# Stick-breaking attention inside a fused encoder block: the layout of the stored values, the order of the first and last steps, and a third output buffer

## The chip, the cores and the metric

The kernel runs on one core of a Trainium2 chip. The metric is the device time of one execution in microseconds (us); the kernel before takes 1874.46 us in the median of three runs (1873.33 to 1877.96).

## What is computed

One layer of an encoder trunk on 1024 tokens of width 1024, in float32. The part that the change touches is branch A, an attention with 16 heads of 64 channels whose weights come from a stick-breaking product instead of a softmax:

```python
h = rmsnorm(x, ln1_g) * (1 + sc1) + sh1
q, k, v, cb, cc, cx, ga, gb = split(h @ w_in)
q, k = rmsnorm(q per head), rmsnorm(k per head)
z = q @ k.T / sqrt(64)                       # strictly causal, s < t
a[t, s] = sigmoid(z[t, s]) * prod_{s < j < t} (1 - sigmoid(z[t, j]))
y_a = a @ v
y_b = cb * causal_dwconv3(cc * cx)
merged = sigmoid(ga) * (y_a @ w_branch_a) + sigmoid(gb) * (y_b @ w_branch_b)
x = x + g1 * (merged @ w_out)
x = x + g2 * swiglu_ffn(rmsnorm(x) * (1 + sc2) + sh2)
```

## The kernel before, in words

Every float32 matrix is split into a high and a low part, and a product is three TensorE (PE) matmuls (high by high, high by low, low by high). The kernel is a row of stages. The first computes the input norm and the projections of v (its first half) and k; then come q, the convolution inputs and the gates; then the attention stage; then branch A's projection, the output projection and the feed-forward part. Most intermediate results go to DRAM and come back (the tiles named `d_...`).

**Attention.** A step is one head and one block of 128 queries, so there are 128 steps, 8 to a head. `att_scores` multiplies queries and keys into PSUM (z, L774 and L775), ScalarE (ACT) takes a sigmoid of the negated score (L776), and VectorE (DVE) forms the running product along the keys with one scan (L780). The attention weight of a key is the difference of two neighbouring running products. The kernel never forms it: it multiplies the running product with the difference of neighbouring value rows, v[t] - v[t-1], and adds the last value. `load_v` (L719 to L725) therefore loads the values twice from DRAM, as `va` (shifted) and `vb`, for two heads at a time; `att_dv` (L727 to L735) subtracts them on DVE (1024 elements in each partition) and splits the difference into `vt`. `att_trans` transposes the running product on PE (L795) and splits it (ACT L798, DVE L799) two steps later; `att_av` multiplies it with `vt` every second step (L810, L811), adds the last value (`vlast`, L815), and DVE puts the sum into the tile `oy` (L817), of which there are two; the SP queue writes it to `d_ya` (L819).

**Values.** `d_v` (L68) holds the values of heads 0 to 7 as 1025 rows of 512 floats, those of heads 8 to 11 and 12 to 15 as 1025 rows of 256; row 0 is zero (L420). A store writes whole rows: 2 KB pieces from `finish_v` (L407, ACT's queue, first stage), 1 KB pieces from the fillers (L889, SP's queue, inside the attention stage). A load takes 128 columns of each row, in pieces of 512 bytes. `load_vlast` reads the last row of each block of 128 into `vl`, in the buffer tagged `va`.

**Fillers.** `fillers` is a generator of matmul work that attention does not need at once: the second half of the v projection (32 pieces of 12 matmuls of 256 columns, L884 to L886), the cb projection and branch B's projection (64 pieces of 6 matmuls of 512 columns each, L865 to L867). Ten pieces (`HEAD`, L941) run ahead of the first step; `fill` (L946) lets the rest through in proportion to the attention work done, up to `FILL - TAIL`, and what is left follows the last value product (`lastav`, L973).

**Order.** The order of each engine's queue is fixed when the program is built: among the instructions that are ready by the planner's timeline, the one of highest priority goes first (`schedule_with_timeline_sim`, L1559). Priority follows the order of the code, and `tc.high_priority()` puts attention ahead of the fillers. `tc.issue_after(x)` adds an edge that keeps the instructions of its block behind x on x's own engine. Every queue then runs strictly in its order: an instruction that waits holds up all that is behind it on its engine. SP issues nearly all loads and stores of the attention stage, ACT's queue those of the first stages.

In step s of `attention()` (L826): the keys and queries of the next head are loaded at the head's first step (L832), `va` and `vb` of the next pair of heads at s % 16 = 10 and 11 (L835 to L837), the difference is formed at s % 8 = 5 or 6 (L838), `load_vlast(1)` stands at s = 54. Before the loop (L954 to L962) come `load_vlast(0)`, the two value loads, the keys of head 0, the first difference, and the ten filler pieces.

Of the kernel before, what the change touches and what calls it, by code (L numbers as in the profile page):

```python
# [16 lines left out]
P = 128  # L17
# [11 lines left out]
def block_kernel(tc, x, x_t, cols, ada_1, ada_2, ada_row, w_q, w_kv, w_v1, w_cg, w_a, w_b, w_o, w_g, w_u, w_d, out):  # L29
# [8 lines left out]
    def nm(s):  # L38
        uid[0] += 1
        return f"{s}_{uid[0]}"  # L40
# [27 lines left out]
    d_v = [drp.tile([T + 1, n], F32, name=f"d_v{n}_{e}") for e, n in enumerate((512, 256, 256))]  # L68
# [310 lines left out]
    def finish_k(ps, i, ch):  # L379
# [13 lines left out]
        hl_ = ap.tile([P, 2, 512], F32R, tag="vs", bufs=3, name=nm("khl"))  # L393
# [7 lines left out]
    def finish_v(ps, i):  # L401
        vs = ap.tile([P, 512], F32, tag=("vs", "qn")[i % 2], bufs=3 - i % 2, name=nm("vs"))
        if i % 2:
            nc.vector.tensor_copy(out=vs, in_=ps)
        else:
            nc.scalar.activation(vs, ps, AF.Copy)
        nc.scalar.dma_start(d_v[0][1 + i * P:1 + (i + 1) * P], vs)  # L407
# [11 lines left out]
    for e in range(3):  # L419
        nc.scalar.dma_start(d_v[e][0:1], mk[0:1, :d_v[e].shape[1]])  # L420
# [298 lines left out]
    def load_v(h, e):  # L719

        pr = h // 2
        d, c0 = (d_v[0], pr * P) if h < 8 else (d_v[1 + (h - 8) // 4], pr % 2 * P)
        t_ = ("vb", "va")[e]
        vab[t_] = bp.tile([P, KT, P], F32, tag=t_, bufs=1, name=nm(t_))
        lastld[0] = nc.sync.dma_start(vab[t_], d[e:T + e, c0:c0 + P].rearrange("(i p) d -> p i d", p=P))  # L725
# [11 lines left out]
    def load_vlast(e):  # L737

        vl = bp.tile([8, 512], F32, tag="va", bufs=1, name=nm("vl"))
        for d, c in (((0, 0),), ((1, 0), (2, 256)))[e]:  # L740
            nc.sync.dma_start(vl[:, c:c + d_v[d].shape[1]], d_v[d][1:].rearrange("(i p) d -> i p d", p=P)[:, P - 1])
        return vl
# [60 lines left out]
    def att_av(h, g):  # L803
# [9 lines left out]
        yv = bp.tile([DH, 256], F32, tag="oy", bufs=2, name=nm("oy"))  # L813
# [12 lines left out]
    def attention():  # L826

        steps = [(h, i) for h in range(H) for i in (LAST if h == H - 1 else ORDER)]
        for s in range(len(steps) + DAV):
            if s < len(steps):  # L830
                h, i = steps[s]
                if s % 8 == (0 if h else 3) and h + 1 < H:  # L832
                    with tc.issue_after(lastld[0].ins):
                        att_load(h + 1)
                if s % 16 in (10, 11) and h + 1 < H:  # L835
                    with tc.issue_after(lastz[0].ins):
                        load_v(h + 1, 11 - s % 16)  # L837
                if s % 8 == (6 if h % 2 else 5) and h + 1 < H:  # L838
                    att_dv(h + 1)
                if s == 54:  # L840
                    with tc.issue_after(lastld[0].ins):
                        vl = load_vlast(1)
                if s == 56:
                    turn_vlast(1, vl)
                yield from att_scores(h, i)
            if s >= DAV:
                h, i = steps[s - DAV]
                if s % 2 != DAV % 2:
                    yield from att_av(h, i // 2)
            if 0 <= s - 2 < len(steps):  # L850
                yield from att_trans(*steps[s - 2])
# [17 lines left out]
    def fillers():  # L869
        for e in range(2):  # L870
# [5 lines left out]
            for i in range(8):  # L876
# [12 lines left out]
                nc.sync.dma_start(d_v[1 + e][1 + i * P:1 + (i + 1) * P], vs)  # L889
# [51 lines left out]
    HEAD, TAIL = 10, 20.0  # L941
# [12 lines left out]
    with tc.high_priority():  # L954
        vl = load_vlast(0)
        turn_vlast(0, vl)
        load_v(0, 1)
        load_v(0, 0)
        att_load(0)
        att_dv(0)  # L960
        for j in range(HEAD):
            next(fl)  # L962
    at_ = attention()
    while True:
# [4 lines left out]
        ta += ca_  # L969
        with tc.issue_after(lastz[0].ins):  # L970
            fill(min(ta * ratio, FILL - TAIL))
    fill(FILL - TAIL)
# [590 lines left out]
```

## Time and profile before

| | before |
|---|---|
| median of 3 runs | 1874.46 us (1873.33 to 1877.96) |
| the profiled execution's own time | 1876.28 us |
| its span, first to last instruction | 1874.5 us |
| PE busy | 1822.7 us, 97% of the span |
| DVE busy | 1351.5 us, 72% |
| ACT busy | 795.0 us, 42% |
| PE's granted clock, mean | 0.990 |
| DMA | 357.98 MB, 191 GB/s in the mean |

Busy PE time is modelled from pipelined matmuls, so a busy PE is not PE at its peak; idle time of PE is real. In a timeline row the columns are the start, the time taken, the engine, the line and operation, what it writes and reads, and in brackets how long the engine stood idle before it and for whom. In a windows row they are the stretch, its length, each engine's busy time with its count of instructions, PE's granted clock (1.00 is full), the mean busy share of the 16 DMA engines and their rate. "x3" is the count of merged instructions. Attention fills the stretch from about 571 to 1040 us.

### The profile page before, as it was taken

To read this page: it belongs to the slowest core of one execution; us is meant where nothing else is said; L and a number is where in the kernel's file an instruction comes from. 1 tells how busy PE (TensorE), PEld (TensorE's weight loads), DVE (VectorE), ACT (ScalarE), POOL (GpSimd) and SP (SyncE) were. 2 spreads that over 40 slices of the span, in tenths; PEclk is the share of its full clock that TensorE was granted. 3 is DMA by queue.
4 is the path that set the end of the run, shared out by engine and by line. 5 is a ranking of instruction groups with operands and counts; after the bars stand their busy time and mean duration, and the time that the engine had idled before them with its cause. 6 is when DMAs were issued, how large, how long until landed. Compare 5 with 4: busy or idle time off the path is not lost. (4 is left out here: it accounts for less than half of the span.)

```text
span 1874.5 us, 24882 instructions
## 1 busy us (share of the span) xinstructions
PE 1822.7 (97%) x8829; PEld 1510.6 (81%) x8829; DVE 1351.5 (72%) x1946; ACT 795.0 (42%) x1494; POOL 369.4 (20%) x277
## 2 busy tenths in 40 slices
PE   7999999999998999998999999989999999999999
PEld 5787778888878988887888888867888888878887
DVE  6873877778963888786888544579987787744776
ACT  4342553333343656555656311564344334422321
POOL 1043328324230000000000000104544454300000
PEclk9999999999999999999999999999999999999999
DMA  9588452226739466678653636424443334388866
GB/s 390 201 306 304 163 174 78 74 99 238 275 135 271 124 191 163 185 189 276 164 162 109 206 125 221 130 79 169 152 185 135 147 146 171 121 317 325 289 225 224
DMA packets 156417, 357.98 MB, mean 191 GB/s; under 512 B 15467, under 2 KB 54653, under 8 KB 154118
## 3 DMA queue, kind: packets, MB, share of 16 engines
q1 hardware_dynamic: 114048, 289.09, 46.2%
q10 hardware_dynamic: 41238, 63.64, 9.7%
q0 software_dynamic: 1008, 3.67, 0.5%
q8 instruction: 70, 1.15, 0.2%
q14 instruction: 53, 0.43, 0.1%
HBM read 245.71 MB, written 110.63 MB: 190 GB/s over the span
## 5 line engine op out<-in xcount | busy, mean ns | idle before, releaser
L780 DVE TENSOR_TENSOR_SCAN pt<-pt,mk 128x128 f32<-128x128 f32 (+7 forms) x128 | 172.1, 1350 | 31.2 <-ACT pt L776 30.8
L776 ACT ACTIVATE pt<-z,rq 128x512 f32<-128x512 f32 (+2 forms) x192 | 108.0, 580 | 95.1 <-PE z L775 62.7
L127 PE MATMUL e<-big,whi 128*128 128x512 f32 x352 | 137.6, 391 | 3.2 <-ACT whi L1056 2.5
L129 PE MATMUL e<-big,wlo 128*128 128x512 f32 x352 | 137.3, 390 | 0.9 <-DVE wlo L1057 0.8
L128 PE MATMUL e<-big,whi 128*128 128x512 f32 x352 | 137.0, 389 | 0.0
L118 POOL TENSOR_SCALAR rs_m<-ss 128x1 f32<-128x1 f32 x8 | 2.2, 281 | 674.3 <-ACT xn L1195 674.3
L132 DVE TENSOR_TENSOR c<-e,c 128x512 f32<-128x512 f32 x138 | 92.8, 687 | 52.6 <-PE e L129 50.8
L127 PE MATMUL pj<-big,whi 128*128 128x512 f32 x320 | 125.2, 391 | 0.5 <-DVE c L132 0.4
L128 PE MATMUL pj<-big,whi 128*128 128x512 f32 x320 | 124.7, 390 | 0.0
L129 PE MATMUL pj<-big,wlo 128*128 128x512 f32 x320 | 124.4, 390 | 0.0
L1390 PE MATMUL e<-whi,f 128*128 128x512 f32 (+1 forms) x319 | 121.8, 382 | 1.5 <-DMA f<-d_f 1.5
L1391 PE MATMUL e<-wlo,f 128*128 128x512 f32 (+1 forms) x319 | 121.8, 382 | 0.0
L1392 PE MATMUL e<-whi,f 128*128 128x512 f32 (+1 forms) x319 | 121.6, 382 | 0.0
L132 DVE TENSOR_TENSOR c<-pj,c 128x512 f32<-128x512 f32 x140 | 93.3, 683 | 33.4 <-PE pj L129 33.2
L290 PE MATMUL pj<-whi,big 128*128 128x512 f32 x352 | 110.7, 401 | 3.1 <-ACT big L273 3.0
L132 POOL TENSOR_TENSOR ws<-raw,raw 128x512 f32<-128x512 f32 x40 | 56.9, 1424 | 288.1 <-DMA raw<-w_cg 145.0
L466 ACT ACTIVATE whi<-raw 128x512 fp32r<-128x512 f32 x116 | 72.5, 630 | 92.1 <-PE pj L128 39.6
L799 DVE TENSOR_TENSOR atl<-tr,ath 128x512 fp32r<-128x512 f32 (+1 forms) x192 | 99.9, 549 | 15.6 <-ACT ath L798 14.1
L132 DVE TENSOR_TENSOR wlo<-raw,whi 128x512 fp32r<-128x512 f32 x116 | 87.5, 759 | 31.9 <-ACT whi L466 31.9
L798 ACT ACTIVATE ath<-tr 128x512 fp32r<-128x512 f32 (+1 forms) x192 | 86.4, 489 | 47.8 <-PE o L810 25.6
L127 PE MATMUL e<-rh,whi 128*128 128x512 f32 x264 | 104.3, 395 | 2.4 <-ACT rh L1073 2.4
L128 PE MATMUL e<-rl,whi 128*128 128x512 f32 x264 | 104.6, 396 | 1.2 <-DVE rl L132 1.2
(255 smaller groups left out, 5043.5 us busy)
## 6 DMA issues: line engine op xcount, KB each, us to landing
f<-d_f SPq DMA_DIRECT2D x77, 512.0 KB, 4.4
d_f<-fs SPq DMA_DIRECT2D x70, 512.0 KB, 3.4
raw<-w_cg SPq DMA_DIRECT2D x40, 512.0 KB, 3.7
raw<-w_u SPq DMA_DIRECT2D x26, 512.0 KB, 3.2
raw<-w_g SPq DMA_DIRECT2D x25, 512.0 KB, 3.4
ad<-ada ACTq DMA_DIRECT2D x19, 512.0 KB, 4.7
ada<-ada SPq DMA_DIRECT2D x8, 1024.0 KB, 9.2
d_t<-ts SPq DMA_DIRECT2D x16, 512.0 KB, 4.9
```

Source lines behind the costliest of these rows:

```text
L127: nc.tensor.matmul(ps, wh[:, k, :], fh[:, k, :], start=(k == 0), stop=False)
L128: nc.tensor.matmul(ps, wh[:, k, :], fl[:, k, :], start=False, stop=False)
L129: nc.tensor.matmul(ps, wl[:, k, :], fh[:, k, :], start=False, stop=(k == 3))
L132: eng.tensor_tensor(out=out, in0=a, in1=b, op=op)
L290: nc.tensor.matmul(ps, a, b, start=(k == 0 and q == 0), stop=(k == KT - 1 and q == 2))
L776: nc.scalar.activation(pt[:, off + s0:off + s0 + m], z[:, :m], AF.Sigmoid, scale=rq[:, 1, i, h:h + 1])
L780: nc.vector.tensor_tensor_scan(out=pt[:, rev], data0=pt[:, rev], data1=mk[:, rev], initial=1.0, op0=ALU.mult, op1=ALU.max)
L798: nc.scalar.activation(th[:, :nb, c0:c0 + P], src, AF.Copy)
L799: nc.vector.tensor_tensor(out=tl[:, :nb, c0:c0 + P], in0=src, in1=th[:, :nb, c0:c0 + P].bitcast(F32), op=ALU.subtract)
L1390: nc.tensor.matmul(o, sh, w[0][:, c], start=(j == 0), stop=False)
L1391: nc.tensor.matmul(o, sh, w[1][:, c], start=False, stop=False)
L1392: nc.tensor.matmul(o, sl, w[0][:, c], start=False, stop=(j == NJ - 1))
```

## The change

The values now lie in DRAM as `d_v[n, 129, 8, 128]`: for each pair of heads, partition p holds in row p + 1 the values of tokens p, 128 + p, 256 + p and so on, 128 floats of each, 4 KB in one piece. A load (`vb` from rows 1 to 128, `va` from rows 0 to 127) is 128 pieces of 4 KB. A store now writes pieces of 512 bytes. Row 0, which `va` needs in partition 0, is a copy of row 128 moved on by one block: `put_before` copies it from DRAM to DRAM on SP's queue, after the last store of each group, three times in all. `vl` gets a buffer of its own, `oy` a third one, and the tiles of the first stage that hold k and half of the v stores a fourth.

Ahead of the loop the keys of head 0 are now loaded first, then the values; the first difference moves to step 2; 16 filler pieces instead of 10 run first, and the rest is thinned (`FILL` less 1.3 for each of the 16, `TAIL` 10). In the loop the value loads stand at s % 16 = 6 and 7, for the pair that follows, and the loads and differences stand in a block tied behind `lastz`, the latest score matmul. After the last step, each yield of the remaining value products and transposes lets one more piece of 1.3 through.

```diff
-    d_v = [drp.tile([T + 1, n], F32, name=f"d_v{n}_{e}") for e, n in enumerate((512, 256, 256))]
+    d_v = [drp.tile([n, P + 1, KT, P], F32, name=f"d_v{n}_{e}") for e, n in enumerate((4, 2, 2))]
...
-        hl_ = ap.tile([P, 2, 512], F32R, tag="vs", bufs=3, name=nm("khl"))
+        hl_ = ap.tile([P, 2, 512], F32R, tag="vs", bufs=4, name=nm("khl"))
...
-        vs = ap.tile([P, 512], F32, tag=("vs", "qn")[i % 2], bufs=3 - i % 2, name=nm("vs"))
+        vs = ap.tile([P, 512], F32, tag=("vs", "qn")[i % 2], bufs=4 - i % 2 * 2, name=nm("vs"))
...
-        nc.scalar.dma_start(d_v[0][1 + i * P:1 + (i + 1) * P], vs)
+        nc.scalar.dma_start(d_v[0][:, 1:, i].rearrange("r p d -> p r d"), vs.rearrange("p (r d) -> p r d", d=P))
...
+    def put_before(e):
+
+        nc.sync.dma_start(d_v[e][:, 0, 1:], d_v[e][:, P, :KT - 1])
+
+    put_before(0)
...
-        d, c0 = (d_v[0], pr * P) if h < 8 else (d_v[1 + (h - 8) // 4], pr % 2 * P)
+        d = d_v[0][pr] if h < 8 else d_v[1 + (h - 8) // 4][pr % 2]
...
-        lastld[0] = nc.sync.dma_start(vab[t_], d[e:T + e, c0:c0 + P].rearrange("(i p) d -> p i d", p=P))
+        lastld[0] = nc.sync.dma_start(vab[t_], d[e:P + e])
...
-        vl = bp.tile([8, 512], F32, tag="va", bufs=1, name=nm("vl"))
+        vl = bp.tile([8, 512], F32, tag="vl", bufs=1, name=nm("vl"))
...
-        yv = bp.tile([DH, 256], F32, tag="oy", bufs=2, name=nm("oy"))
+        yv = bp.tile([DH, 256], F32, tag="oy", bufs=3, name=nm("oy"))
...
         for s in range(len(steps) + DAV):
+            flush[0] = s >= len(steps)
             if s < len(steps):
...
-                if s % 16 in (10, 11) and h + 1 < H:
-                    with tc.issue_after(lastz[0].ins):
-                        load_v(h + 1, 11 - s % 16)
-                if s % 8 == (6 if h % 2 else 5) and h + 1 < H:
-                    att_dv(h + 1)
+                with tc.issue_after(lastz[0].ins) if s else ExitStack():
+                    if s == 2:
+                        att_dv(0)
+                    if s % 8 == (6 if h % 2 else 5) and h + 1 < H:
+                        att_dv(h + 1)
+                    if s % 16 in (6, 7) and s + 16 < len(steps):
+                        load_v(2 * (s // 16) + 2, 7 - s % 16)
...
-                nc.sync.dma_start(d_v[1 + e][1 + i * P:1 + (i + 1) * P], vs)
+                nc.sync.dma_start(d_v[1 + e][:, 1:, i].rearrange("r p d -> p r d"), vs.rearrange("p (r d) -> p r d", d=P))
+                if i == 7:
+                    put_before(1 + e)
...
-    HEAD, TAIL = 10, 20.0
+    HEAD, TAIL = 16, 10.0
+    FILL -= 1.3 * HEAD
...
         turn_vlast(0, vl)
+        att_load(0)
         load_v(0, 1)
         load_v(0, 0)
-        att_load(0)
-        att_dv(0)
         for j in range(HEAD):
             next(fl)
     at_ = attention()
+    flush, nfl = [0], 0
     while True:
...
         ta += ca_
+        nfl += flush[0]
         with tc.issue_after(lastz[0].ins):
-            fill(min(ta * ratio, FILL - TAIL))
-    fill(FILL - TAIL)
+            fill(min(ta * ratio, FILL - TAIL) + 1.3 * nfl)
```

More of the change, by code (lines that the diff above doesn't have):

```diff
@@ L419, in block_kernel @@
     for e in range(3):
-        nc.scalar.dma_start(d_v[e][0:1], mk[0:1, :d_v[e].shape[1]])
+        n = d_v[e].shape[0]
+        nc.scalar.dma_start(d_v[e][:, 0:1, 0].rearrange("r p d -> p r d"), mk[0:1, :n * P].rearrange("p (r d) -> p r d", d=P))
+    def put_before(e):
+        nc.sync.dma_start(d_v[e][:, 0, 1:], d_v[e][:, P, :KT - 1])
+    put_before(0)
     def more():
@@ L737, in load_vlast @@
     def load_vlast(e):
-        vl = bp.tile([8, 512], F32, tag="va", bufs=1, name=nm("vl"))
+        vl = bp.tile([8, 512], F32, tag="vl", bufs=1, name=nm("vl"))
         for d, c in (((0, 0),), ((1, 0), (2, 256)))[e]:
-            nc.sync.dma_start(vl[:, c:c + d_v[d].shape[1]], d_v[d][1:].rearrange("(i p) d -> i p d", p=P)[:, P - 1])
+            n = d_v[d].shape[0]
+            nc.sync.dma_start(vl[:, c:c + n * P].rearrange("i (r d) -> i r d", d=P), d_v[d][:, P].rearrange("r i d -> i r d"))
         return vl
```

## The prediction

> **What bounds the kernel now.** The page comes first, to see whether one engine carries the span.
>
> ```profile
> span 1874.5 us, 24882 instructions
> PE 1822.7 (97%) x8829; PEld 1510.6 (81%) x8829; DVE 1351.5 (72%) x1946; ACT 795.0 (42%) x1494; POOL 369.4 (20%) x277
> ```
>
> PE does, and the change removes no matmul, so all it can win is time in which PE stands idle or runs slow: idle is 1874.5 - 1822.7 = 51.8 us. The windows view of the attention stage and PE's waits in it say how much lies there and for whom PE stood.
>
> ```profile
> 560.00:600.00 40.00, 34.89 (x225) 31.79 (x224) 10.27 (x15) 9.32 (x20) 0.00 (x0) 0.96 0.86 252
> 600.00:1040.00 440.00, 424.35 (x2615) 370.63 (x2614) 363.44 (x502) 263.80 (x605) 0.00 (x0) 0.99 0.62 178
> ...
> PE tr L795 <- DVE atl L799: 7.8, 10, 2.5
> PE o L810 <- DVE oy L817: 6.4, 6, 2.9
> PE z L774 <- DMA skh<-d_k: 5.0, 1, 5.0
> ```
>
> That is 5.1 and 15.7 us of idle PE, nearly all under three names. PE's timeline places them; the first two rows are the first and last of the ten filler pieces that run ahead of attention, the last two the first and last filler matmul behind the last value product.
>
> ```profile
> 575.48 0.36 PE L884 MATMUL pj<-whi,big 128*128 128x256 f32 x1
> ...
> 590.37 0.28 PE L886 MATMUL pj<-whi,big 128*128 128x256 f32 x1
> 595.64 0.52 PE L774 MATMUL z<-skh,sqt 128*128 128x128 f32 x2 [5.00 <-DMA skh<-d_k]
> ...
> 788.76 0.33 PE L795 MATMUL tr<-dm,pt 128*128 128x128 f32 x1 [2.46 <-DVE atl L799]
> ...
> 858.52 0.39 PE L810 MATMUL o<-ath,vt 128*128 128x256 f32 x1 [1.29 <-DVE oy L817]
> ...
> 872.98 0.55 PE L810 MATMUL o<-ath,vt 128*128 128x256 f32 x1 [2.95 <-DVE oy L817]
> ...
> 946.70 0.66 PE L795 MATMUL tr<-dm,pt 128*128 128x128 f32 x4 [1.54 <-DVE atl L799]
> ...
> 1027.48 0.66 PE L795 MATMUL tr<-dm,pt 128*128 128x128 f32 x4 [0.84 <-DVE atl L799]
> ...
> 1031.34 0.39 PE L810 MATMUL o<-ath,vt 128*128 128x256 f32 x1 [1.72 <-DVE oy L817]
> 1033.66 0.73 PE L865 MATMUL pj<-big,whi 128*128 128x512 f32 x1
> ...
> 1041.51 0.39 PE L867 MATMUL pj<-big,wlo 128*128 128x512 f32 x1
> ```
>
> A gap can cost more than its length: windows laid behind the gaps show the granted clock.
>
> ```profile
> 595.64:599.40 3.76, 3.64 (x17) 3.42 (x18) 1.12 (x2) 1.01 (x3) 0.00 (x0) 0.55 1.09 392
> 788.76:792.76 4.00, 4.00 (x21) 3.38 (x21) 3.94 (x7) 2.91 (x7) 0.00 (x0) 1.00 0.49 131
> 872.98:880.30 7.32, 7.32 (x32) 6.54 (x32) 3.77 (x7) 3.07 (x8) 0.00 (x0) 0.57 0.87 323
> 1032.40:1036.40 4.00, 4.00 (x17) 3.46 (x16) 2.83 (x5) 2.83 (x6) 0.00 (x0) 0.57 0.49 174
> 586.00:594.00 8.00, 4.65 (x39) 4.44 (x38) 2.52 (x3) 1.53 (x3) 0.00 (x0) 1.00 1.06 221
> ```
>
> Behind the gaps of 5.00 and 2.95 and behind the pair 0.84 and 1.72 the clock is near half: lost are 0.45 x 3.76 = 1.7, 0.43 x 7.32 = 3.1 and 0.43 x 4.00 = 1.7 us. Behind 2.46 it is full.
>
> **The head: keys first, 16 pieces (won 6.7, given back 1.5).** Ten pieces take 590.65 - 575.48 = 15.2 us, 1.5 each, and then the first score waits 5.0 us for keys. SP's timeline says why they are late:
>
> ```profile
> 571.68 0.40 SPq L725 DMA_DIRECT2D vb<-d_v  x1
> ...
> 582.46 0.38 SPq L725 DMA_DIRECT2D va<-d_v  x1
> ```
>
> Both value loads lie among the key loads, and all 16 DMA engines are full (share 1.06) at only 221 GB/s, against 392 GB/s a few us later. Six more pieces are 9.1 us of work, so the score would have to come after 599.7 us to leave a gap; with keys ahead of values it is ready sooner. The pieces are moved and not added, so the 9.1 us leave the steps; gap and slow clock go: 5.0 + 1.7 = 6.7. New is that the first half of the fillers ends with the 16th piece, and the first steps need pieces of the second half, whose weights must be loaded and split by then. If they come late PE idles: 0 to 6.7. I take 1.5, near the 1.72 of the tail, where attention also lacks pieces.
>
> **A buffer of its own for vl (2.5, back 0.7).** DVE's rows:
>
> ```profile
> 786.76 1.22 DVE L132 TENSOR_TENSOR vb<-vb,va 128x1024 f32<-128x1024 f32 x1 [4.20 <-DMA va<-d_v]
> ...
> 858.04 0.43 DVE L817 TENSOR_TENSOR oy<-o,otmp 64x256 f32<-64x256 f32 x1 [3.79 <-DMA d_ya<-oy]
> ...
> 872.41 0.43 DVE L817 TENSOR_TENSOR oy<-o,otmp 64x256 f32<-64x256 f32 x1 [4.03 <-DMA d_ya<-oy]
> ...
> 942.64 1.23 DVE L132 TENSOR_TENSOR vb<-vb,va 128x1024 f32<-128x1024 f32 x1 [2.79 <-DMA vb<-d_v]
> ```
>
> The 4.20 us is the one wait of the loop for `va`, whose buffer `vl` held, and PE's gap of 2.46 stands 2 us behind it. It goes; next late is `vb`, as at the other pairs, so I give back 0.7 (0 to 1.54, the gap after 942.64).
>
> **Third oy (7.4, back 1.0).** The waits of 3.79 and 4.03 are for a store that must free one of two buffers; with three, the store that counts lies two steps (over 6 us, 128 steps in some 440 us) further back. Won are 1.29 + 2.95 and the slow clock, 3.1. DMA is near full there (0.87), so something else may be late next: back 1.0 (0 to 7.4).
>
> **Products between the last steps (4.3, back 1.2).** 0.84 + 1.72 + 1.7. Before, the fillers left for after the last value product last 1033.66 to 1041.7, 8.1 us; after, six yields of 1.3 are let through before it and about 2.2 units remain. The cover that this takes away hid a chain: the last splits of `ya`.
>
> ```profile
> 1056.37 0.69 DVE L132 TENSOR_TENSOR ya<-yr,ya 128x512 fp32r<-128x512 f32 x1 [2.23 <-ACT ya L1007]
> ```
>
> It ends at 1057.06, 15.3 us after the fillers, when PE works on `ya` already: that chain is next late if PE gets there sooner. But the pieces now lie ahead of that work, not away from it, and 14.3 units are left at step 128 where 11.5 were (attention's last 4.73 units times the old and new ratio, plus 7 and 10). So 1.2 back (0 to 4.3).
>
> **Layout, tie and eight steps (0.5).** Three rows show that the loads cannot come earlier:
>
> ```profile
> 656.95 0.68 DVE L132 TENSOR_TENSOR vt<-vb,vt 128x512 fp32r<-128x512 f32 x1
> 657.66 0.37 SPq L725 DMA_DIRECT2D vb<-d_v  x1
> 663.26 0.42 DVE L780 TENSOR_TENSOR_SCAN pt<-pt,mk 128x128 f32<-128x128 f32 x1
> ```
>
> This load stands in the code at step 27, under the same tie; it is issued when the last reader frees `vb`, before the scan of step 24. The tie names a PE matmul and binds only what PE issues, so it held neither this load nor will it hold a difference, which DVE runs. What is left is the faster landing.
>
> ```profile
> raw<-w_cg SPq DMA_DIRECT2D x40, 512.0 KB, 3.7
> vb<-d_v SPq DMA_DIRECT2D x8, 512.0 KB, 4.4
> ...
> d_k<-khl ACTq DMA_DIRECT2D x32, 256.0 KB, 6.1
> ...
> d_v<-vs SPq DMA_DIRECT2D x16, 128.0 KB, 5.2
> ```
>
> 4.4 against 3.7 for the same bytes in 4 KB pieces: 0.7 of the 2.79 that DVE waits is a quarter of PE's gap of 1.54 behind it, 0.4; I take 0.5 with the smaller ones (0 to 1.54). The Trainium skill, DMA: Bandwidth & Descriptors, Specifications, calls 512 bytes enough for line rate; by that the layout wins nothing and the sum is 0.5 less. The trace disagrees: 221 against 392 GB/s with the engines full.
>
> **Thinner fillers (-3.0).** Six pieces less lie in the steps, 9.1 us, and some 418 us (440 less 9.1 and the 13.0 below) then hold the 363 us of DVE work that 440 held: 87% against 83%. PE's short waits for DVE that nothing above touches are 7.8 - 2.46 - 1.54 - 0.84 = 3.0; I let them double (0 to 12.5, one wait of 0.78 at each of 16 heads).
>
> **Stores and copies (-1.0).** Stores in 512-byte pieces should land more like `d_k`, whose pieces are as small: 6.1 against 5.2. In the head, eight stores share four buffers. Each `put_before` stands on SP until the last store has landed, with key loads, filler weights and `d_ya` stores behind it. SP already stands so without PE noticing; in the first stage PE has little to lose to anything.
>
> ```profile
> SPq L725 <- DVE vt L132: 20.2, 6, 5.9
> ...
> L290 PE MATMUL pj<-whi,big 128*128 128x512 f32 x352 | 110.7, 401 | 3.1 <-ACT big L273 3.0
> ```
>
> The cover is one head of slack, since keys are loaded a head ahead; without it a copy could cost what late keys cost, 5.0. I take 1.0 (0 to 5). The fourth buffer there wins nothing.
>
> **Sum.** 6.7 - 1.5 + 2.5 - 0.7 + 7.4 - 1.0 + 4.3 - 1.2 + 0.5 - 3.0 - 1.0 = 13.0 us. The profiled execution took 1876.28 (span 1874.5), within the three runs and 1.8 above their median; taken from the median 1874.46 it gives 1861.5.
>
> **Rivals.** (1) The head starves: PE's gap only moves behind the 16th piece, since stores or the second half's weights are late. For it: the engines are full from 586 to 600. Against: the keys need not wait for values. The head's 5.2 is lost: 1866.7. (2) Another wait replaces that for `oy`: 6.4 lost, 1867.9. For it: DMA share 0.87; against: no other DMA wait of PE stands there. (3) The tie does hold the differences behind scores: then the rest of the 1.54 and of PE's other small waits, some 2.3, go too, 1859.2; the row at 657.66 speaks against it. (4) The slow clock does not hang on the short gaps, so filling 2.95, 0.84 and 1.72 does not bring back 3.1 + 1.7: 1866.3. The Trainium skill, TensorE: Matmul & The Clock Gate, Why this matters for your kernels, speaks of gaps above about 3 us; the trace shows near half clock behind smaller ones. (5) Slower: with thin fillers DVE sets the step. PE waits 0.78 (7.8 over 10) twice a head, at its two longest scans: 32 x 0.78 = 25, where 3 is in the sum, so 1861.5 + 22 = 1883.5. It decides the sign from (13 + 3) / 0.78, about 20 waits; before has ten. DVE's 87% speaks for it, ACT's 60% and the few waits now against.
>
> **How the numbers follow.** Forecast 0.46, rivals 0.13, 0.12, 0.10, 0.09 and 0.10 in that order. Low end: all that is named is won, 20.9 + 1.5, 1852, set to 1853. High end: rivals 1 and 2 together, 1873, set to 1872, which leaves out rival 5 and little more. A measurement of this kernel tells some 0.3% from no change, so faster is below 1868.8: nearly all of the forecast and of rival 3, two thirds of 1, 2 and 4, 0.75. Same, up to 1880.1: 0.16, the rest of these and a little of 5. Slower: 0.09.
>
> **What would show it.** Right: no gap at the first score, granted clock 1.00 at 595 to 600; no DVE wait for `va` in the loop; none of `oy` for `d_ya` above 1 us; no PE gap between the last two value products; `vb` landing near 3.7 but still issued when `vt` frees it, and differences still early. Wrong: a new PE gap of over 3 us with a clock near 0.5 behind it, above all at 599 to 612, or PE's waits for `atl` at over 16 us in sum.

## The result and the profile after

The changed kernel takes 1862.18 us in the median of four runs (1861.12 to 1865.98), the kernel before 1875.92 beside it (four runs, 1873.33 to 1877.96): a ratio of 0.9938, 95% interval 0.9916 to 0.9960. Measured again later it was 0.9945 (0.9923 to 0.9967); of those executions one, of 10,337 us, is left out. Forecast were 1861.5 us, 13.0 less than before; the ratio stands for 11.6 us, 7.5 to 15.8.

The page after, the attention stage, PE's waits from 540 to 1060 us and DVE's from 600 to 1020:

```profile
span 1860.6 us, 24885 instructions
PE 1815.7 (98%) x8829; PEld 1505.1 (81%) x8829; DVE 1351.7 (73%) x1946; ACT 794.0 (43%) x1494; POOL 369.3 (20%) x277
```

```profile
560.00:600.00 40.00, 39.25 (x270) 35.93 (x268) 13.62 (x20) 12.54 (x28) 0.00 (x0) 1.00 0.81 249
600.00:1040.00 440.00, 431.67 (x2652) 376.92 (x2650) 369.97 (x512) 266.14 (x608) 0.00 (x0) 1.00 0.64 187
```

```profile
PE tr L803 <- DVE atl L807: 5.4, 11, 0.8
PE pj L876 <- DVE sgi L1036: 3.9, 1, 3.9
PE pj L876 <- ACT ya L1021: 1.1, 1, 1.1
...
PE o L818 <- DVE oy L825: 0.6, 4, 0.2
```

```profile
DVE vb L132 <- DMA vb<-d_v: 2.3, 3, 1.8
```

Idle time of PE fell from 51.8 to 44.9 us, and its busy time, for the same 8829 matmuls, by 7.0. That is about what the mean granted clock accounts for: 0.010 x 1874.5 = 18.7 us lost before, 0.006 x 1860.6 = 11.2 after. The waits for keys and for `oy` are gone. New is a wait for `sgi` (the gate of branch A, loaded for its projection), behind attention. The timeline places head and tail:

```profile
587.26 0.40 PE L782 MATMUL z<-skh,sqt 128*128 128x128 f32 x2
...
1017.43 0.39 PE L876 MATMUL pj<-ya,whi 128*128 128x512 f32 x1
...
1037.97 0.50 PE L876 MATMUL pj<-ya,whi 128*128 128x512 f32 x1 [1.07 <-ACT ya L1021]
...
1043.29 0.80 PE L876 MATMUL pj<-ya,whi 128*128 128x512 f32 x1 [3.86 <-DVE sgi L1036]
...
1116.28 0.40 PE L1188 MATMUL e<-whi,big 128*128 128x512 f32 x1
```

```profile
1043.29:1047.99 4.70, 4.70 (x11) 3.77 (x12) 3.63 (x6) 1.26 (x2) 0.00 (x0) 0.51 0.51 162
```

The first score has no bracket: no gap. Behind the 3.86 the clock is half, 2.3 us lost. This is a sign that the prediction had named as wrong, a new PE gap of over 3 us with a clock near 0.5 behind it, though not where it expected one. The first product of the output projection starts at 1116.28; before:

```profile
1129.17 0.40 PE L1174 MATMUL e<-whi,big 128*128 128x512 f32 x1
```

**A measure for the experiments.** The first filler piece started at 572.4 to 576.8 us in the profiles of this study, though nothing ahead of it differs enough for that: two executions of the changed kernel had 575.85 and 572.58. So kernels are compared by what is called **the stretch** below: the time from the first filler piece to the first product of the output projection, which holds all that the change touches but the stores of the first stage: 1129.17 - 575.48 = 553.7 us before, 1116.28 - 575.85 = 540.4 after. From its end to the end of the kernel it is 745.3 and 744.3. Two columns explain the stretch: the PE gaps of 0.3 us and more between 560 and 1060 us, and the slow clock behind gaps, read from windows of 3 to 5 us as 1 less the granted clock, times the length.

| kernel | ratio to before (interval) | stretch | PE gaps | slow clock |
|---|---|---|---|---|
| before | 1 | 553.7 | 19.3 | 6.5 |
| changed | 0.9938 (0.9916 to 0.9960) | 540.4 | 10.2 | 2.3 |
| changed, again | 0.9945 (0.9923 to 0.9967) | 538.1 | 7.2 | 1.7 |
| before, new head alone | 0.9954 (0.9938 to 0.9971) | 544.8 | 11.7 | 4.9 |
| before, third oy alone | 0.9990 (0.9976 to 1.0004) | 551.2 | 17.8 | 6.3 |
| changed, old head | 1.0012 (0.9997 to 1.0027) | 551.8 | 18.0 | 5.2 |
| changed, two oy | 0.9981 (0.9964 to 0.9999) | 546.1 | 14.2 | 3.3 |
| changed, vl in va's buffer | 0.9970 (0.9952 to 0.9988) | 545.6 | 11.0 | 5.7 |
| changed, old layout | 0.9931 (0.9904 to 0.9958) | 540.6 | 9.9 | 1.5 |
| changed, old end | 0.9935 (0.9919 to 0.9951) | 538.2 | 8.6 | 1.5 |
| changed, w_o behind row 2 | 0.9929 (0.9913 to 0.9946) | 536.0 | 7.9 | 0 |
| the same, old end | 0.9952 (0.9927 to 0.9977) | 540.8 | 11.2 | 1.7 |
| changed, w_o behind row 5 | 0.9941 (0.9922 to 0.9961) | 536.7 | 8.4 | 0 |
| changed, tie on DVE | 0.9937 (0.9917 to 0.9958) | 536.7 | 7.5 | 1.7 |

In every row the stretch is that of before less what gaps and slow clock fell by, within 1.3 us: before has 25.8 of both, changed 12.5, and 553.7 - 13.3 = 540.4. So the account leaves out nothing larger than 1.3 us; gaps under 0.3 us, 1.6 to 3.3 us in sum, are not in it. Each row is one profiled execution. Two executions of the changed kernel differ by 2.4 us in the stretch, so a smaller difference between two profiles tells nothing.

**One execution and many.** The profiled execution of the kernel before is one of its slower ones. Lost to the clock over the whole kernel (1 less the mean granted clock, times the span) are some 19 us in it, but 15.2 in the mean of the 59 executions of that kernel that were timed beside the experiments; for the changed kernel it is 11.4 in the profile and 11.6 in the mean of nine. So the execution that was profiled before lost about 4 us more to the clock than that kernel does in the mean, and the 13.3 us between the two profiles may hold some of it; how much of it falls into the stretch is not known. The mean times of the same executions, 1871.7 and 1861.7 us on several chips, differ by 10.0.

### The profile page after: what moved, and what is told of

The parts are those of the page before. It is cut to its first block, busy times and chain, and to the rows that moved or that the text cites. A ratio compares the mean times of both kernels' runs of the same rounds, so it can differ in the third digit from the quotient of the medians.

```text
span 1860.6 us, 24885 instructions
## 1 busy us (share of the span) xinstructions
PE 1815.7 (98%) x8829; PEld 1505.1 (81%) x8829; DVE 1351.7 (73%) x1946; ACT 794.0 (43%) x1494; POOL 369.3 (20%) x277
## 5 line engine op out<-in xcount | busy, mean ns | idle before, releaser
L784 ACT ACTIVATE pt<-z,rq 128x512 f32<-128x512 f32 (+3 forms) x192 | 107.1, 579 | 88.6 <-PE z L783 57.5
L806 ACT ACTIVATE ath<-tr 128x512 fp32r<-128x512 f32 (+1 forms) x192 | 86.8, 489 | 44.0 <-PE o L818 25.8
```

The source lines that it names most:

```text
L784: nc.scalar.activation(pt[:, off + s0:off + s0 + m], z[:, :m], AF.Sigmoid, scale=rq[:, 1, i, h:h + 1])
L806: nc.scalar.activation(th[:, :nb, c0:c0 + P], src, AF.Copy)
```

## The experiments

The theory was that of the prediction: parts with a price each, of which the head, `vl`, `oy` and the end carry the gain. The rivals were that another wait takes the place of the one removed, and that the layout or the tie carries more than it was given. "Theory A" and the like below are those of the expectation just above.

**The new head alone**, in the kernel before:

```diff
         turn_vlast(0, vl)
+        att_load(0)
         load_v(0, 1)
         load_v(0, 0)
-        att_load(0)
-        att_dv(0)
...
-    HEAD, TAIL = 10, 20.0
+    HEAD, TAIL = 16, 7.0
+    FILL -= 1.3 * HEAD
```

with the first difference at step 2.

> The kernel before with the head alone changed: keys loaded ahead of the values, 16 filler pieces ahead of attention in place of ten, the first difference at step 2; what runs behind the last value product is that of before. Theory (the prediction's head term): the gap of 5.00 us at the first score and the half clock behind it go, 6.7 us won, up to 1.5 back: 5.2 to 6.7 us less than before. Rival (the head starves): the gap moves behind the 16th piece, within 1.5 us of before. Rival (the gap only lets the rest catch up and is given back at the oy and atl waits): 0 to 3 us less.

Measured: 0.9954, 8.6 us less, 8.9 in the stretch: more than the theory, but not where it had it. A new gap stands in the head, 2.82 us with a slow clock behind it, for the first difference, whose `vb` lands late and which holds up the scan behind it:

```profile
590.98 1.22 DVE L132 TENSOR_TENSOR vb<-vb,va 128x1024 f32<-128x1024 f32 x1 [5.34 <-DMA vb<-d_v]
```

```profile
592.86 0.47 PE L795 MATMUL tr<-dm,pt 128*128 128x128 f32 x1 [2.82 <-DVE pt L780]
```

and the window behind it:

```profile
592.86:596.86 4.00, 4.00 (x20) 3.81 (x21) 3.79 (x6) 2.01 (x6) 0.00 (x0) 0.59 1.07 305
```

The head itself won 6.7 - 2.82 - 1.6 = 2.3. The rest is mainly that PE's two gaps for `oy`, 1.29 and 2.95, and the clock behind, 7.3 in all, did not occur, with two `oy` still; against that, the wait for `va` cost PE more (gaps of 2.59 and 1.51 and 1.7 of clock, where before it was 2.46). The likely reason, not shown, is that where a store lands late depends on what other transfers it meets, and the head had moved all of them.

**The third oy alone**, in the kernel before:

```diff
-        yv = bp.tile([DH, 256], F32, tag="oy", bufs=2, name=nm("oy"))
+        yv = bp.tile([DH, 256], F32, tag="oy", bufs=3, name=nm("oy"))
```

> The kernel before with a third oy buffer and nothing else. Theory: the waits of 1.29 and 2.95 us go and with the longer one the half clock of 3.1 us behind it: 7.3 us won, up to 1.0 back, so 6.4 to 7.4 less than before. Rival (the slow clock does not hang on such short gaps): 3.2 to 4.2 less. Rival (another wait takes the place): 1 us or less.

Measured: 0.9990, no difference that can be told. The rival holds. No gap for `oy` is left in the loop; but a DVE that does not stand for `oy` reaches the next difference earlier, and waits there for `vb`, 5.81 us where before it was 2.62:

```profile
889.09 1.23 DVE L132 TENSOR_TENSOR vb<-vb,va 128x1024 f32<-128x1024 f32 x1 [5.81 <-DMA vb<-d_v]
```

```profile
893.15 0.47 PE L795 MATMUL tr<-dm,pt 128*128 128x128 f32 x1 [3.04 <-DVE atl L799]
```

and the window behind it:

```profile
893.15:897.10 3.95, 3.95 (x18) 3.66 (x19) 3.89 (x9) 0.47 (x1) 0.00 (x0) 0.61 1.07 270
```

PE's gap moved from 872.98 to 893.15 and kept its length; the slow clock behind it costs half as much, 1.5. The remaining difference is in places where a third `oy` has no part: a wait for keys of 5.60 and more slow clock behind it and behind a gap of 2.42 cost this execution 3.1 us, and full clock behind the 1.72 at the end saved it 1.7.

**Single parts undone in the changed kernel.** First the head:

```diff
-        att_load(0)
         load_v(0, 1)
         load_v(0, 0)
+        att_load(0)
+        att_dv(0)
...
-                    if s == 2:
-                        att_dv(0)
...
-    HEAD, TAIL = 16, 10.0
+    HEAD, TAIL = 10, 10.0
```

> The changed kernel with the head of before: both value loads ahead of the keys, the first difference there too, ten filler pieces. Theory A (the prediction's head term): a gap of about 5 us at the first score and 1.7 us of half clock, 5 to 7 us slower than the changed kernel. Theory B (4 KB rows let the values land sooner and the keys behind them too): a gap of 2 us or less, within 2 us of the changed kernel. Theory C (part of the gap is given back later, since DVE and the loads catch up in it): the gap is there, and the time within 3 us of the changed kernel.

```profile
599.47 0.45 PE L782 MATMUL z<-skh,sqt 128*128 128x128 f32 x1 [10.32 <-DMA skh<-d_k]
```

and the window behind it:

```profile
599.47:603.40 3.93, 3.50 (x15) 3.21 (x16) 1.81 (x3) 1.09 (x3) 0.00 (x0) 0.50 0.96 309
```

1.0012: all of the gain is lost, 11.4 us of the stretch, twice theory A. The gap is 10.32 in place of 5.00. Both value loads are issued here ahead of any key (570.14 and 570.61 us), where before one of them went between the keys (571.68 and 582.46); and with loads eight steps ahead, those of the next pair stand between the keys too (583.67 and 586.15). Which of the two lengthens the gap was not tried. Short rows are not to blame. From 582 to 590 us, with all 16 engines full in both, the transfers of the kernel before and of this one are

```profile
DMA packets 1440, 1.84 MB, mean 230 GB/s; under 512 B 97, under 2 KB 1121, under 8 KB 1439
```

```profile
DMA packets 580, 1.94 MB, mean 242 GB/s; under 512 B 107, under 2 KB 107, under 8 KB 580
```

With 4 KB rows there are 2.5 times fewer packets and the rate is 5% higher. The head was slow because of the order in which bytes were asked for, and not because of their pieces. In every kernel with the keys first the first score runs 11.4 us after the first filler piece (587.26 - 575.85), sooner than ten pieces end (15.2): the order alone closes the gap, and the six more pieces were not needed for it.

Then `oy`, with two buffers:

```diff
-        yv = bp.tile([DH, 256], F32, tag="oy", bufs=3, name=nm("oy"))
+        yv = bp.tile([DH, 256], F32, tag="oy", bufs=2, name=nm("oy"))
```

> The changed kernel with two oy buffers in place of three. Theory A (the prediction's term of 7.4, back 1.0): the waits for d_ya's stores and PE's gaps behind them come back, 4 to 7 us slower. Theory B (with the head changed and two buffers the two PE gaps for oy did not occur, so they hung on where the stores fell among other transfers): within 1 us of the changed kernel, with DVE waiting for d_ya under 2 us at a time and no PE gap for oy above 1 us before the last value product.

```profile
834.27 0.43 DVE L825 TENSOR_TENSOR oy<-o,otmp 64x256 f32<-64x256 f32 x1 [3.44 <-DMA d_ya<-oy]
```

```profile
834.84 0.46 PE L818 MATMUL o<-ath,vt 128*128 128x256 f32 x1 [3.19 <-DVE oy L825]
```

and the window behind it:

```profile
834.84:838.80 3.96, 3.96 (x17) 3.73 (x18) 3.48 (x6) 1.90 (x6) 0.00 (x0) 0.57 1.03 412
```

5.7 us slower in the stretch, of which 3.19 + 0.68 of gaps and 0.43 x 3.96 = 1.7 of clock: theory A. In this kernel no other wait takes the place. That the gap stands at 834 and not at 858 and 873 fits a place that hangs on the other transfers.

Then `vl`, back in `va`'s buffer:

```diff
-        vl = bp.tile([8, 512], F32, tag="vl", bufs=1, name=nm("vl"))
+        vl = bp.tile([8, 512], F32, tag="va", bufs=1, name=nm("vl"))
```

> The changed kernel with vl in va's buffer again. Theory A (the prediction's term): DVE waits 4 to 6 us for va near 786 us, PE 2.5 us near 788, and in some executions near half clock stands behind it: 2.5 to 4 us slower than the changed kernel. Theory B (with loads in 4 KB rows the load of va lands early enough even behind vl): within 1 us.

5.1 us slower in the stretch, above theory A, and by another path: it is not DVE that waits, for `va`, but PE itself, for `vl`.

```profile
772.26 1.20 DVE L132 TENSOR_TENSOR vb<-vb,va 128x1024 f32<-128x1024 f32 x1
```

```profile
773.49 0.29 SPq L749 DMA_DIRECT2D vl<-d_v  x1
```

```profile
778.80 0.19 PE L755 MATMUL tr<-dm,vl 8*64 8x8 f32 x1 [1.88 <-DMA vl<-d_v]
```

and the window behind it:

```profile
778.80:782.80 4.00, 4.00 (x27) 3.79 (x28) 2.02 (x3) 1.76 (x4) 0.00 (x0) 0.64 0.80 251
782.80:786.80 4.00, 4.00 (x15) 3.31 (x15) 1.22 (x3) 1.25 (x3) 0.00 (x0) 0.51 0.78 299
```

With loads eight steps ahead, `va` of the next pair takes the shared buffer before `vl` does, so `vl` is issued only when the difference has read it (772.26 + 1.20), 56 us later than in the changed kernel (717.77). The gap of 1.88 costs 1.88 + 0.36 x 4.00 + 0.49 x 4.00 = 5.3.

Then the layout, with array, stores and loads of before and no copies; of its lines the two that carry it:

```diff
-    d_v = [drp.tile([n, P + 1, KT, P], F32, name=f"d_v{n}_{e}") for e, n in enumerate((4, 2, 2))]
+    d_v = [drp.tile([T + 1, n], F32, name=f"d_v{n}_{e}") for e, n in enumerate((512, 256, 256))]
...
-        lastld[0] = nc.sync.dma_start(vab[t_], d[e:P + e])
+        lastld[0] = nc.sync.dma_start(vab[t_], d[e:T + e, c0:c0 + P].rearrange("(i p) d -> p i d", p=P))
```

> The changed kernel with the value rows of before: stores, loads and the array in 512-byte pieces, no copy of the rows that precede. Theory A (the prediction's terms: layout 0.5 won, stores and copies 1.0 paid): within 1 us of the changed kernel. Theory B (the kernels with one part alone showed DVE waiting for vb 2.2 to 5.8 us with the old rows, and 1.8 at most with the new): the vb waits come back, with one or two PE gaps of 1.5 to 3 us, some of them with 1.7 us of half clock behind: 2 to 6 us slower than the changed kernel. In the profile the two differ in the sum of DVE's waits for vb from 600 to 1020 us: under 4 us by A, 6 to 13 by B.

0.9931 and a stretch of 540.6: nothing, theory A. DVE's waits for `vb` are 4.5 us in sum, a little above the 4 of that theory (2.3 and 3.3 in the two profiles of the changed kernel), and no PE gap comes of them.

**The end of attention.** The old end in the changed kernel:

```diff
-    HEAD, TAIL = 16, 10.0
+    HEAD, TAIL = 16, 7.0
...
-            fill(min(ta * ratio, FILL - TAIL) + 1.3 * nfl)
+            fill(min(ta * ratio, FILL - TAIL))
+    fill(FILL - TAIL)
```

> The changed kernel with the old end of attention: no products let through between the last value products, 7 units kept for after them. Theory: the changed end costs what its trace shows, waits of 1.07, 0.22 and 3.86 us and 2.3 us of half clock, 7.5 in all, where the end of before cost 4.3; so the old end is 3 us faster than the changed kernel, 1859 us. Rival (the prediction's term): the products between the last steps are worth 3.1 us, and this kernel is 3 us slower, 1865 us. Rival (both ends wait for the same chain of loads of ya, sga and mb, the one a little earlier than the other): within 1 us of the changed kernel.

0.9935: no difference from the changed kernel that the runs can tell, as the third case had it, but not for its reason. The end itself has the gaps of 0.84 and 1.72 us, the latter with a full clock behind it this time, and no wait for `sgi`; in the loop stand two gaps that the changed kernel has not, 1.28 and 2.20:

```profile
835.63 0.69 PE L803 MATMUL tr<-dm,pt 128*128 128x128 f32 x2 [2.20 <-DVE atl L807]
...
1017.68 0.39 PE L818 MATMUL o<-ath,vt 128*128 128x256 f32 x1 [1.72 <-DVE oy L825]
```

and the window behind it:

```profile
1017.68:1021.60 3.92, 3.92 (x25) 3.58 (x26) 2.31 (x4) 2.82 (x6) 0.00 (x0) 1.00 0.46 156
```

The lower `TAIL` lets more filler work into the steps, which is the likely cause: ahead of 835.63 DVE runs without a pause from 828.82, four pieces of fillers' work among its own. From 600 to 1010 us the gaps come to 5.7 us and 1.5 of clock, against 4.5 and none in the changed kernel.

At the end itself the comparison goes the other way, over kernels that differ elsewhere too. Over the four profiles with the old end (before, the two with one part alone, this one) gaps and clock there cost 4.3, 4.3, 2.6 and 2.6 us; over the seven with the new end and w_o (below) in its old place 7.2, 4.0, 6.7, 6.2, 6.9, 5.2 and 4.2. There the new end costs 2.3 us more in the mean, and by this one pair it wins about as much in the loop. Why it waits is a chain of loads:

```profile
1028.29 0.43 SPq L1033 DMA_DIRECT2D mb<-d_mb  x1
...
1035.18 0.43 SPq L1031 DMA_DIRECT2D sgi<-d_sga  x1
```

```profile
1032.53 0.68 DVE L1037 TENSOR_TENSOR sgi<-sgi,mb 128x512 f32<-128x512 f32 x1
1033.91 0.69 DVE L1042 TENSOR_TENSOR big<-sgi,big 128x512 fp32r<-128x512 f32 x1
...
1042.54 0.69 DVE L1036 TENSOR_TENSOR sgi<-pj,sgi 128x512 f32<-128x512 f32 x1 [3.90 <-DMA sgi<-d_sga]
```

The first `mb` load comes at 1028.29; the sum that needs it frees `sgi` at 1034.6; the `sgi` load of a later product goes at 1035.18 and DVE has it at 1042.54; PE, with both PSUM buffers of `pj` full, waits. The products between the last steps are in part products on `ya` (1017.43, ahead of the last value product), so PE stands at this chain sooner than its loads are.

Which wait holds the first `mb` load? The early loads of the output projection's weights (w_o) through one buffer stand on SP before it, the last of them at 1027.32 with one `yr` load between. They were moved behind the `mb` load of the second row of products:

```diff
         if m == KT - 2:
-            preload_wo()
+            with tc.issue_after(lastmb):
+                preload_wo()
...
-            nc.sync.dma_start(mb, d_mb[m, :, n * 512:(n + 1) * 512])
+            dmb = nc.sync.dma_start(mb, d_mb[m, :, n * 512:(n + 1) * 512])
+            if m == 1:
+                lastmb = dmb.ins
```

> The changed kernel with one thing moved: the early loads of the output projection's weights (w_o, three of 512 or 256 KB through one buffer) are queued on SP behind the mb load of the second row of the w_a products, in place of between the loads of ya. Theory: the third of them stands on SP until its buffer is free (issued at 1027.32 us) and holds the yr and mb loads behind it; the first mb comes at 1028.29, the sums that need it at 1032.53, and sgi, which these free, at 1035.18, for which DVE and then PE wait until 1043.29. Without it the waits of 1.07 and 3.86 and the 2.3 us of half clock go, 4 to 7 us less than the changed kernel: 1855 to 1858. Rival (the two sgi buffers shared with the fillers alone hold the chain): within 1 us of the changed kernel. Rival (w_o then comes late to the output projection): slower than the changed kernel by 2 us or more.

0.9929 looked like the theory (gaps of 0.66, 0.78 and 1.62 us, no slow clock). Two more kernels say more: the same with the old end (the two diffs above together), and the same with w_o behind the fifth row, out of the way altogether:

```diff
-            if m == 1:
+            if m == 4:
```

> The changed kernel with the output projection's early weight loads queued later, as in the run before, and the old end of attention (7 units kept for behind the last value product, none let through before). Theory A: the old end keeps its gaps of 0.84 and 1.72 us but has no wait for yr, sga or mb behind, so it ends within 1 us of the run with only the loads moved, 1858. Theory B: the products between the last steps are worth the 2.6 us and a clock loss of up to 1.7 once the loads come in time: 2.5 to 4.3 us slower than that run.

> The changed kernel with the output projection's early weight loads queued behind the mb load of the fifth row of the w_a products. Theory A (what held the loads of mb, sga and yr was w_o's load on SP): as with the second row or better, PE's waits behind the last value product 3 us or less in sum, no half clock there, 4 to 7 us less than the changed kernel from the first filler piece to the first output-projection product. Rival (mb waits for its three buffers and for the fillers' last stores anyway): waits of 4 us or more remain, within 2 us of the changed kernel.

The first took 0.9952, theory B's size, but less than half of it at the end (0.84, 1.72 and new gaps of 1.50 and 1.25, 5.3 us against 3.1); the rest are the 1.28 and 2.04 in the loop that come with the old `TAIL`. The second has no w_o load anywhere near. By the sum of its gaps and its clock it passes as theory A (2.8 us at the end, full clock); its stretch is 3.8 us shorter than that of the changed kernel, just under the 4 of that theory, and 1.4 shorter than in the second execution of it (next). But the wait itself is there, with the same chain ahead of it and the `mb` load directly behind the store of the last filler's result:

```profile
1030.94 0.35 SPq L949 DMA_DIRECT2D d_mb<-mb  x1
1031.63 0.32 SPq L1034 DMA_DIRECT2D mb<-d_mb  x1
```

```profile
1030.22 0.69 DVE L948 TENSOR_TENSOR mb<-pj,sgi 128x512 f32<-128x512 f32 x1
```

```profile
1042.64 0.50 PE L876 MATMUL pj<-ya,whi 128*128 128x512 f32 x1 [2.27 <-DVE sgi L1039]
```

And the second execution of the changed kernel, with w_o in its old place, has the same wait, 2.29. So the theory that w_o holds the chain falls: it was in front of the chain, but the chain is as late without it. What the load stands behind then is in the rows: DVE finishes the fillers' last result at 1030.22 + 0.69 = 1030.91, SP issues its store at 1030.94, and the `mb` load comes next without a wait of its own. Whether moving it wins a microsecond or two, these runs do not tell from nothing.

**The changed kernel once more**, unedited:

> The changed kernel itself, once more, beside the three others on one chip. Theory (the waits are set by the order of the queues and the buffers): the same small PE waits of 0.68 to 0.82 us at every second head, the same wait of about 3 to 4 us for sgi in the end, 1860 to 1864 us. Rival (they fall by chance in each execution): other waits at other heads, as the granted clock behind a gap of 1.7 us did.

The waits at every second head return at the same places and lengths (0.82 at 753.99 and 805.71, 0.68 at 857.93), so they are set by the queues, as the theory had it. The wait at the end is not so fixed: 2.29 for `sgi` in place of 3.86.

```profile
1038.18 0.50 PE L876 MATMUL pj<-ya,whi 128*128 128x512 f32 x1 [2.29 <-DVE sgi L1036]
```

```profile
1031.93 0.32 SPq L1031 DMA_DIRECT2D sgi<-d_sga  x1
```

```profile
1037.44 1.29 DVE L1036 TENSOR_TENSOR sgi<-pj,sgi 128x512 f32<-128x512 f32 x2 [2.33 <-DMA sgi<-d_sga]
```

Counted from the start of the stretch the load of `sgi` is issued at the same time in both executions (1031.93 - 572.58 = 459.35 and 1035.18 - 575.85 = 459.33). But here DVE goes on 5.5 us after its issue, there 7.4 (1042.54 - 1035.18). So the end's wait has two parts: a late issue, which the queues set, and the load's own time, which differs from one execution to the next.

**A tie that holds.** The tie to `lastz` does not hold a difference. That of heads 2 and 3 stands in the code at step 14, tied behind the last score matmul of step 13 (768 keys, the last 256 of them at 621.83). In the changed kernel's trace it runs 17 us before that matmul:

```profile
604.55 1.22 DVE L132 TENSOR_TENSOR vb<-vb,va 128x1024 f32<-128x1024 f32 x1
```

```profile
621.83 0.28 PE L783 MATMUL z<-skl,sqt 128*128 128x256 f32 x1
```

All seven differences behind the first start like this, 6 to 19 us ahead of the score they are tied to. In the next kernel the difference is tied to the last scan, an instruction of its own engine (the value loads lose their tie with it):

```diff
                     if s % 8 == (6 if h % 2 else 5) and h + 1 < H:
-                        att_dv(h + 1)
+                        with tc.issue_after(lastscan[0].ins):
+                            att_dv(h + 1)
```

> The changed kernel with the differences truly held behind the last scan, by a tie to an instruction of DVE in place of one of PE. Theory A (the tie as written does nothing, and with the loads of this kernel nothing waits for a difference that stands early): within 1 us of the changed kernel. Theory B (the differences still stand early, and PE's regular waits of 0.7 to 0.8 us for atl come of it): 2 to 5 us faster, with PE's waits for atl under 3 us in sum where the changed kernel has 5.4. Theory C (held differences free vb later, and the next load comes late): DVE waits for vb above 4 us in sum and the kernel is slower by 1 us or more.

The tie holds: the same difference now follows the scan of step 13 (624.63).

```profile
626.31 1.20 DVE L132 TENSOR_TENSOR vb<-vb,va 128x1024 f32<-128x1024 f32 x1
```

0.9937: theory A. DVE's waits for `vb` from 600 to 1020 us are gone, and PE's waits for `atl` are the same 5.1 us in sum, at the same heads:

```profile
757.36 0.33 PE L804 MATMUL tr<-dm,pt 128*128 128x128 f32 x1 [0.82 <-DVE atl L808]
```

This one stands behind a scan of 640 elements that DVE runs first, in both kernels alike; no difference is near.

## Why the prediction was right, and where it was wrong

The sum was right, 13.0 forecast and 11.6 measured (13.3 in the stretch of the profiled executions). Most of what was to show it did: no gap at the first score, a clock of 1.00 there, no wait for `va`, none of `oy` above 0.2 us, `vb` still issued when `vt` frees it (649.72, behind the split that began at 649.01), differences still early. Two signs were not as forecast: the new gap of 3.86 at the end, and the landing of `vb`, which was to come near 3.7. The profile has the landing of one of its eight loads alone, 6.3 us, in the full head.

That the total came out was in part luck. Place by place, gaps and slow clock of the two profiles differ by 6.2 us in the head, 2.5 at the wait for `va`, 7.3 at those for `oy`, -3.0 at the end and 0.4 elsewhere, where 5.2, 1.8, 6.4, 3.1 and -3.5 were forecast. The end missed by 6.1; give-backs that did not come (2.6) and costs that did not come (3.9) made up for it. And the prices of the clock, 6.5 us in sum, were read from one execution, which over the whole kernel lost about 4 us more to it than the mean. By its terms:

- **Head: 6.7 less 1.5.** The gap and its clock went as priced, and next to nothing came back at the 16th piece (no gap over 0.4 us in the profile): rival 1 is out. That the sixteen pieces must cover the keys, until 599.7, was wrong: with the keys first the score is ready by 587.26. And the head's worth was more. Undone in the changed kernel it costs 11.4 us, since without it the gap is 10.32; alone it wins 8.9, mostly in waits further on. The prediction gave the gap one price, and it has one for each order of the loads.
- **vl: 2.5 less 0.7.** The wait for `va` is gone, as forecast; the buffer was not tried alone in the kernel before. Shared again in the changed kernel it costs 5.1, by PE's own wait and the clock behind it. The step priced the buffer without the loads eight steps ahead, with which a shared buffer costs more.
- **Third oy: 7.4 less 1.0.** 5.7 in the changed kernel, near nothing alone. Rival 2 is what happens to the part by itself: DVE arrives earlier at the next late load. It fails in the whole change, where DVE waits 1.8 us for `vb` at most.
- **Products between the last steps: 4.3 less 1.2.** This is the step that failed. "So 1.2 back" took the splits of `ya` as next late; they cost 1.07 + 0.22, but the loads of `mb` and `sgi` 3.86 and 2.3 of clock. At the end a loss of about 2.3 stands in place of 3.1 won; with what the other rate of fillers wins in the loop, the new end is worth nothing that the runs can tell.
- **Layout, tie, eight steps: 0.5.** The size is right: 0.2 in the stretch and nothing in the runs for the layout, nothing for the tie, and rival 3 is out, since a tie that holds wins nothing either. The reason for it is not: the faster landing, 4.4 down to 3.7, rested on the three loads of eight whose landing the profile has, and no run shows it. And the argument against the layout being worthless, 221 against 392 GB/s, fails: where the old head ran at 230 with all engines full, it runs at 242 with 4 KB rows. The Trainium skill, DMA: Bandwidth & Descriptors, Specifications, holds that 512 bytes are enough for line rate; the trace agrees, in that rows eight times as long gave 5%, while the 392 GB/s of a few us later was not reached with either.
- **Thinner fillers: -3.0.** Too much: the waits for `atl` that nothing else touches were 3.0 and are 5.4, so 2.4, and none is over 0.82. DVE's share rose to 369.97 of 440, 84%, not 87%: PE ran ahead with less idle, and rival 5 never came near.
- **Stores and copies: -1.0.** No PE wait stands at a copy. One of 0.39 stands at a filler's store (598.24, for `vs`); with the old layout it is 0.32. So nothing was paid. (The 6.1 against 5.2 us that spoke for a cost compared transfers of 256 KB with transfers of 128 KB.)
- **The clock, rival 4.** The slow clock does hang on gaps this short: without it the account of the stretches would be off by up to 6.5 us. The Trainium skill, TensorE: Matmul & The Clock Gate, Why this matters for your kernels, warns of gaps above about 3 us; here the trace differs, with half clock behind 1.72 to 2.42 in most cases. The last section says on what it hangs.

What the runs teach beyond the sum is that the parts do not add up. Undone one by one they cost 11.4 + 5.7 + 5.1 = 22.2 us of the stretch, where all of it is worth 13.3 (by the ratios 13.9, 8.0 and 6.0, where all of it is worth 11.6); alone two of them win 8.9 and 2.5. They stand on one chain of loads, DVE and PE, and each exposes or hides the next.

Three things stay open because they were not tried: what the end would take with the first `mb` load issued ahead of the fillers' last store, and what the loads' step and the six more pieces are worth alone. Open are also why the load of `sgi` takes 5.5 us in one execution and 7.4 in another, and whether any version here beats the changed kernel: the best ratio, 0.9929, lies within the intervals of the changed kernel's own.

## What to carry to other kernels

Price a wait with the slow clock behind it, from more than one execution, and name the next late load before counting the gain: a buffer that removes a wait may only bring its engine sooner to that load, as the third `oy` did alone. Before work is pulled forward to fill a gap, check that the data of what then comes first (here `mb` and `sgi`) is pulled forward too. When two parts share a chain, undo each in the whole as well as trying it alone.

## What the runs showed of the hardware

Whether the clock falls behind a short gap is not settled by its length. Over all profiles it stayed full behind 1.28, 1.54, 1.62, 2.27 and 2.46 us, and was half behind 1.88, 1.92, 2.04, 2.20, 2.26, 2.29 and 2.42; behind the same 1.72, with the same 0.84 some 3 us ahead of it, it was half twice and full three times. Behind gaps of 2.58 us and more (twelve, up to 10.32; one, of 2.59, had another of 1.51 right behind) it always fell.

The traces show what it hangs on. In each of the 14 the granted clock is either 1.00 or 0.50, and a slow period lasts 3.41 us, or two or three times that (the last of an execution is cut by its end). The 0.57 to 0.72 of some windows above are one such period inside a longer window. Within an execution all slow periods begin on one grid of 3.41 us; where the grid lies differs between executions. Two gaps at the wait for `va`, of nearly one length, show what that does when the traces are cut at the grid. With the third `oy` alone, the gap of 2.42 falls into one period, of which PE is busy 1.21 us, and the next one is slow:

```profile
787.00:790.42 3.42, 1.21 (x10) 0.90 (x8) 1.76 (x2) 2.03 (x6) 0.00 (x0) 1.00 0.03 8
790.42:793.83 3.41, 3.20 (x9) 2.69 (x10) 3.38 (x6) 1.96 (x4) 0.00 (x0) 0.50 0.52 154
```

In the kernel before, the gap of 2.46 falls across a border, with 0.75 us idle in one period and 1.71 in the next, and the clock stays full:

```profile
783.64:787.05 3.41, 2.66 (x20) 2.26 (x18) 0.29 (x1) 2.23 (x6) 0.00 (x0) 1.00 0.52 145
787.05:790.47 3.42, 1.71 (x9) 1.50 (x10) 3.39 (x5) 1.23 (x4) 0.00 (x0) 1.00 0.28 66
790.47:793.88 3.41, 3.41 (x20) 2.84 (x19) 3.35 (x6) 2.59 (x6) 0.00 (x0) 1.00 0.38 112
```

It is the same with the 1.72. Before, all of it lies in one period (1029.41 to 1032.82), and the next is slow; with the old end in the changed kernel 0.84 and 1.72 leave 1.10 and 1.45 us idle in two neighbouring periods (from 1012.82 and 1016.23), and the clock stays full. Over the 14 whole executions (from 40 us on, idle time by the modelled ends of matmuls) the period behind one at full clock was slow in all 46 cases with over 1.9 us idle, in none of 7315 with under 1.5, and in 13 of the 33 between. One slow period costs 1.7 us where PE is busy through it. So a gap of about 2 us costs either itself or, as at 778.80, nearly three times itself, and of two executions of one kernel one may pay and the other not.
